# A two-layer trunk on one core: the products within chunks of its state-space mixer, issued for two chunks at once

## The chip, the core and the metric

The kernel runs on one core of a Trainium2 chip. The metric is the device time of one launch in microseconds (us); less is better. Time before: 2029.46 us, the median of 3 runs (2022.63 to 2030.07).

TensorE (PE; its weight loads are PEld) multiplies, VectorE (DVE) and ScalarE (ACT) and GpSimd (POOL) work on tiles in between, SyncE (SP) issues most transfers. Each engine takes its instructions in a fixed order; engines wait for each other by semaphores.

## What is computed

Layer 0 is a bidirectional state-space mixer (Mamba-2 form) on 256 context and 1024 latent tokens, layer 1 an attention mixer; each is wrapped in a normalisation with a modulation and a gated residual. The change lies in the mixer's scan, which splits the 1280 tokens into 10 chunks of 128. Cut to what matters:

```python
def ssd_scan(xs, dt, a, bm, cm, init_state, need_y=True):
    ...
    la_cum = jnp.cumsum(dtc * a, axis=2)
    ...
    causal = jnp.tril(jnp.ones((M_CHUNK, M_CHUNK), dtype=bool))[:, :, None, None]
    seg = la_cum[:, :, :, None] - la_cum[:, :, None, :]
    decay = jnp.exp(jnp.where(causal, seg, -jnp.inf))
    cb = jnp.einsum('bclgn,bcsgn->bclsg', cc, bc)
    w = cb[..., None] * decay * dtc[:, :, None]
    y_diag = jnp.einsum('bclsgr,bcsgrp->bclgrp', w, xc)
    y_off = jnp.einsum('bclgn,bcgrpn,bclgr->bclgrp', cc, prev, jnp.exp(la_cum))
    return (y_diag + y_off).reshape(xs.shape), final
```

`y_diag` is the product within chunks: for each chunk, group (8) and head (4 per group) a 128 x 128 matrix `w` times the chunk's inputs (64 columns per head). Both directions of the scan share `cb` and the inputs, so the kernel adds the two directions' decay matrices first and multiplies once.

## The kernel before, in words

The mixer's stage interleaves two streams. One projects: 48 tiles of 128 output columns, each in three blocks of tokens (256, 512, 512), in eight steps of the inner dimension, each step as three matmuls of operands split into a high and a low part (L168 to L170, tile `pj`). A convolution tile is evicted by ScalarE into `ub` (L636), goes through five taps on ScalarE and VectorE (L642, L645) and a Silu (L650). The other stream is `mix`, once per group when its four convolution tiles are there. For each of the 10 chunks it

- transposes inputs and B (`trans`, L690, tile `tc`) and copies them to `xst` and `Bt`;
- makes chunk states (`state`): GpSimd weighs the inputs (`xw`, L713), TensorE multiplies (L718, tile `st`), GpSimd and VectorE carry them on (`tm`, `PV`);
- makes the decay matrix (`wmat`): SP brings the cumulated logarithms per direction (`lab`, L750), GpSimd masks them (L754), ScalarE takes four exponentials per direction (L760, tile `W`), TensorE makes the cross product C times B (L770, tile `tc`), VectorE adds the directions (L773) and multiplies by the cross product (L775);
- multiplies the matrix with `xst` (`diag`, L791, tiles `yd`): four heads of 64 columns.

After the last chunk of a block of tokens (`inner`, L805) VectorE adds `yd` to the skipped inputs; `y_out` (L832, tile `yo`) adds what comes from earlier chunks and stores `y_d`, the input of the output projection.

The order on every engine is made ahead by `Plan.order`: a list scheduler with a rank, a planned duration and the engine for each step. A step starts at the earliest planned time at which the steps it needs have ended and its buffers are free; of those that could start, the lowest rank goes first. The steps of `mix` have ranks ahead of later projections. Buffers are counted as rings, taken in turn: `W0` and `W1` (the two directions' decay matrices) have two buffers each, `lab` three, `tc` two banks, `yd` one set of two banks per block of tokens. A `W0` buffer is taken by the first exponential of its direction and comes free when `diag` has ended (W0 also holds the sum), `W1` after the addition L773. What comes out is a fixed sequence per engine; on the chip an engine waits where the planned and the real durations differ.

Of the kernel before, what the change touches and what calls it, by code (L numbers as in the profile page):

```python
# [133 lines left out]
def tok0(c):  # L134
    return c * 128 + (2 if c >= 2 else 0)
# [6 lines left out]
def flat(ap):  # L142
    return ap.rearrange("p a b -> p (a b)")


def emit(tc, A, out):
    nc = tc.nc
    V, S, G, T, Q = nc.vector, nc.scalar, nc.gpsimd, nc.tensor, nc.sync
# [90 lines left out]
    def psum(tag, shape):  # L239
        return PS.tile(shape, FT, tag=tag, bufs=PSN[tag], name=tag)  # L240
# [424 lines left out]
    def mix(g, chs, rank):  # L665
# [6 lines left out]
        def op(eng, f, after, us, **kw):  # L672
            seq[0] += .01
            return plan.op(eng, f, after, rank + seq[0], us, **kw)

        s = {}
        hxst, hBt, hPV = plan.hold("xst"), plan.hold("Bt"), plan.hold("PV")
        ready, blocks = {}, {}
# [22 lines left out]
            d = op("ACT", lambda: S.activation(s["Bt"][:, c, :], t["p"][:, 2, :], AF.Copy), [a], .275, uses=[bank, hBt])  # L701
            ready[c] = (b, d)

        pv = [None]

        def state(i):
            bank, t, mms = plan.hold("st"), {}, []
# [31 lines left out]
        def wmat(c):  # L739

            t0, t, ws, bank = tok0(c), {}, [], plan.hold("tc")
            for d in range(2):
                hl, hw = plan.hold("lab"), plan.hold(f"W{d}")
                sgn = 1 - 2 * d

                def bring(d=d):
                    t["l", d] = pool["now"].tile([128, 4, 128], FT, tag="lab", bufs=NLAB, name="lab")
                    src = bass.AP(tensor=la_d.tensor, offset=la_d.offset + (c * 64 + d * 32 + g * 4) * 128,
                                  ap=[[0, 128], [1, 512]])
                    Q.dma_start(flat(t["l", d]), src)  # L750


                def close(d=d, sgn=sgn):
                    G.affine_select(t["l", d], t["l", d], [[0, 4], [sgn, 128]], OP.is_ge, NEVER, base=0,  # L754
                                    channel_multiplier=-sgn)

                def expo(h, d=d):
                    if h == 0:
                        t["w", d] = pool["now"].tile([128, 4, 128], FT, tag=f"W{d}", bufs=2, name="W")
                    S.activation(t["w", d][:, h], t["l", d][:, h], AF.Exp, bias=u_t[:, d, c, 4 * g + h:4 * g + h + 1])  # L760

                a = op("SP", bring, third + [la_op], .38, takes=[hl])
                a = op("POOL", close, [a], .88, uses=[hl])
                for h in range(4):
                    a = op("ACT", lambda h=h, f=expo: f(h), [a, u_op], .312, takes=[hw] if h == 0 else [], uses=[hl, hw], table="exp")
                ws.append((hw, a))

            def cross():
                t["cb"] = psum("tc", [128, 128])
                T.matmul(t["cb"], bt["a"][:, t0:t0 + 128], ct["a"][:, t0:t0 + 128], start=True, stop=True)  # L770

            b = op("PE", cross, [ab, ac], .22, takes=[bank], uses=[hb, hc])
            a = op("DVE", lambda: V.tensor_tensor(t["w", 0], t["w", 0], t["w", 1], op=OP.add), [w[1] for w in ws], .75,  # L773
                   uses=[w[0] for w in ws])
            a = op("DVE", lambda: V.tensor_tensor(t["w", 0], t["w", 0], t["cb"][:, None, :].to_broadcast([128, 4, 128]),  # L775
                                                  op=OP.mult), [a, b], .68, uses=[ws[0][0], bank])
            bi = [i for i, (c0, c1) in enumerate(BLOCKS) if c0 <= c < c1][0]
            if bi not in blocks:
                blocks[bi] = {"h": plan.hold("yd"), "ops": [], "c": BLOCKS[bi]}
                new = True  # L780
            else:
                new = False
            bk = blocks[bi]
            k = (c - bk["c"][0]) * 128

            def diag():
                if new:
                    bk["yd"] = [psum("yd", [128, 512]) for q in range(2)]
                for h in range(4):
                    q, j = divmod(h, 2)  # L790
                    T.matmul(bk["yd"][q][j * 64:(j + 1) * 64, k:k + 128], s["xst"][:, c, h, :], t["w", 0][:, h, :], start=True,  # L791
                             stop=True)

            bk["ops"].append(op("PE", diag, [a, ready[c][0]], .65, takes=[bk["h"]] if new else [], uses=[bk["h"], ws[0][0], hxst]))

        def inner(bi):

# [63 lines left out]
        for i in range(9):  # L861
            state(i)
            wmat(i)
            if i == 1:
                inner(0)
            if i == 5:
                inner(1)
        wmat(9)
        for q in range(2):
            y_out(0, q)  # L870
# [78 lines left out]
    for kind, g, q in ORDER:  # L949
        rank += 10  # L950
        if kind == "z":
            z_tile(next(zts), rank)
            continue
        chs.setdefault(g, []).append(conv_tile((2 * g, 2 * g + 1, 16 + g, 24 + g)[q], rank))
        mod_later(g, q, rank + LATE)
        if q == 3:
            mix(g, chs[g], rank + 1)
# [18 lines left out]
    with ExitStack() as st:  # L976
# [262 lines left out]
        a = plan.op("SP", norm_weights, [opened], HEAD, us=.76, small=True)  # L1239
# [3 lines left out]
        for i in range(2):  # L1243
# [9 lines left out]
            c = [plan.op("POOL", cosines, [scaled, b, *tabs], HEAD + 20 + 40 * i, 1.1)]  # L1253
# [299 lines left out]
    with ExitStack() as st:  # L1553
# [18 lines left out]
        held, shifts, brought, finished, last_scores, turns = {}, {}, {}, {}, [], []  # L1572
# [155 lines left out]
        for kt in range(KT):  # L1728
            for h in range(2):
                raw, t = plan.hold("wr"), {}  # L1730
                c = slice(h * 512, (h + 1) * 512)
# [10 lines left out]
                a = plan.op("SP", bring, [], R - 80 if kt < WE else 100 * NU - 150 + kt, takes=[raw])  # L1742
                a = plan.op("ACT", lambda t=t, f=part: S.activation(f(0), t["w"], AF.Copy), [a] + after, R, .63, uses=[raw])
# [151 lines left out]
```

## Time and profile before

| | us |
|---|---|
| median of 3 runs | 2029.46 |
| lowest and highest run | 2022.63, 2030.07 |
| the profiled execution | 2022.52 |
| its span, first to last instruction | 2020.8 |
| TensorE busy in it | 1959.8 (97%) |
| VectorE busy | 1433.7 (71%) |
| GpSimd busy | 1192.1 (59%) |
| ScalarE busy | 1109.0 (55%) |

The profile is of one execution. Busy time of TensorE counts each matmul from start to end, where neighbours overlap, so gaps shorter than a matmul's tail do not show as idle; start times in the timeline do show them. Mixer work with the changed products lies between 204 and 1004 us, the last projection of the stage at 1029, then the output projection and the attention layer follow.

### The profile page before, as it was taken

How to read it: one execution, taken by the hardware profiler on the slowest of the kernel's cores; microseconds unless marked ns; L12 is line 12 of the kernel's file. 1: busy time of each engine (PE TensorE's matmuls, PEld its weight loads, DVE VectorE, ACT ScalarE, POOL GpSimd, SP SyncE). 2: the span in 40 equal slices, each digit the busy share in tenths (PEclk: the TensorE clock that was granted, in tenths of full speed). 3: DMA queues.
4: the chain of work that ended last, by engine and by line, in shares of the span. 5: the costliest groups of instructions: out<-in, count | busy, mean ns of one | idle time of the engine just before them, and what ended most of it. 6: DMA issues, size and time to landing. Idle time of an engine off the chain costs nothing.

```text
span 2020.8 us, 30740 instructions
## 1 busy us (share of the span) xinstructions
PE 1959.8 (97%) x10728; PEld 1495.2 (74%) x10728; DVE 1433.7 (71%) x1737; ACT 1109.0 (55%) x2037; POOL 1192.1 (59%) x973
## 2 busy tenths in 40 slices
PE   8899999999999999999999999999998999999998
PEld 8778887888888888788878878887774444444476
DVE  1485888786959686776455788767574888888643
ACT  2447868576776668575644776543224445544521
POOL 1202767675847574755459787864264667776722
PEclk9999999999999999999999999999999999999999
DMA  6104455535363546354486685462233111111033
GB/s 243 63 32 127 142 171 149 155 98 170 113 189 102 157 118 175 123 147 153 140 277 213 214 257 188 155 180 94 74 94 89 32 37 43 48 43 37 6 103 105
DMA packets 163151, 255.51 MB, mean 126 GB/s; under 512 B 22490, under 2 KB 58202, under 8 KB 162996
## 3 DMA queue, kind: packets, MB, share of 16 engines
q1 hardware_dynamic: 161844, 251.71, 40.8%
q8 instruction: 84, 1.38, 0.3%
q10 hardware_dynamic: 1152, 1.84, 0.2%
q14 instruction: 71, 0.58, 0.1%
HBM read 210.78 MB, written 42.63 MB: 125 GB/s over the span
## 4 chain that ended last, share of the span: by engine, by line
PE 80%; DVE 7%; DMA 4%; ACT 3%; issue 2%; POOL 2%; SPq 1%; DVEq 0%; POOLq 0%; ACTq 0%
PE pj L168 9%; PE pj L169 8%; PE pj L170 8%; PE sc L1658 7%; PE ot L1674 7%; PE ob L168 7%; PE ob L170 7%; PE ob L169 7%; DVE acc L645 3%; PE yo L832 3%; PE st L718 3%; PE sc L1457 2%; PE yd L791 2%; DMA spare<-in_mod_w 2%; PE sc L168 1%
## 5 line engine op out<-in xcount | busy, mean ns | idle before, releaser
L168 PE MATMUL pj<-inh,whi 128*128 128x512 f32 (+1 forms) x1152 | 440.5, 382 | 3.9 <-DVE dv L453 3.2
L169 PE MATMUL pj<-inl,whi 128*128 128x512 f32 (+1 forms) x1152 | 409.7, 356 | 0.8 <-POOL inl L367 0.8
L170 PE MATMUL pj<-inh,wlo 128*128 128x512 f32 (+1 forms) x1152 | 410.4, 356 | 0.0
L754 POOL TENSOR_SCALAR_AFFINE_SELECT lab<-lab 128x512 f32<-128x512 f32 x160 | 150.6, 948 | 174.0 <-DMA lab<-la_d 135.3
L645 DVE SCALAR_TENSOR_TENSOR acc<-ub,convw,acc 128x1282 f32<-128x1282 f32 x128 | 232.5, 1817 | 18.8 <-ACT acc L642 15.8
L168 PEld LDWEIGHTS pj<-inh,whi 128*128 128x128 f32 x1152 | 219.0, 190 | 33.8 <-DVE dv L453 3.6
L170 PEld LDWEIGHTS pj<-inh,wlo 128*128 128x128 f32 x1152 | 218.3, 189 | 32.2
L169 PEld LDWEIGHTS pj<-inl,whi 128*128 128x128 f32 x1152 | 219.2, 190 | 26.2 <-POOL inl L367 1.2
L1639 POOL TENSOR_TENSOR acc<-acc,P 128x1024 f32<-128x1024 f32 x80 | 192.2, 2403 | 67.1 <-ACT P L1663 65.8
L1663 ACT ACTIVATE P<-sc 128x1024 f32<-128x1024 f32 x160 | 163.1, 1026 | 122.6 <-PE sc L1658 106.3
L760 ACT ACTIVATE W<-lab,u_t 128x128 f32<-128x128 f32 x640 | 201.4, 390 | 38.9 <-POOL lab L754 31.5
L1604 DVE TENSOR_REDUCE mx<-sc 128x2 f32<-128x1024 f32 (+1 forms) x140 | 167.4, 1214 | 40.9 <-PE sc L1457 39.9
L713 POOL TENSOR_TENSOR xw<-xst,te_t 128x256 f32<-128x256 f32 x144 | 142.0, 1003 | 43.0 <-DVE xst L697 16.5
L1674 PE MATMUL ot<-P,vv 128*64 128x512 f32 x640 | 156.5, 610 | 0.0
L1658 PE MATMUL sc<-q,kh 64*128 64x512 f32 x640 | 136.2, 422 | 6.5 <-ACT P L1663 3.9
L602 POOL TENSOR_TENSOR wlo<-wraw,whi 128x512 fp32r<-128x512 f32 x48 | 69.0, 1438 | 110.5 <-ACT whi L599 110.4
L1658 PEld LDWEIGHTS sc<-q,kh 64*128 64x128 f32 x640 | 60.2, 185 | 76.7 <-DVE mx L1604 29.5
L170 PE MATMUL ob<-whi,yl 128*128 128x512 f32 x288 | 113.4, 394 | 1.8 <-DVE yl L1056 1.4
L168 PE MATMUL ob<-whi,yh 128*128 128x512 f32 x288 | 113.9, 395 | 0.0
L169 PE MATMUL ob<-wlo,yh 128*128 128x512 f32 x288 | 112.9, 392 | 0.0
L732 POOL TENSOR_TENSOR tm<-PV,dec_t 128x512 f32<-128x512 f32 x64 | 97.0, 1515 | 25.4 <-DVE PV L736 25.4
L836 DVE TENSOR_TENSOR es<-yo,es 128x512 f32<-128x512 f32 (+1 forms) x96 | 53.2, 554 | 80.3 <-PE yo L832 44.5
(281 smaller groups left out, 4536.1 us busy)
## 6 DMA issues: line engine op xcount, KB each, us to landing
lab<-la_d SPq DMA_DIRECT2D x160, 256.0 KB
wraw<-in_w_in SPq DMA_DIRECT2D x96, 256.0 KB
workvv<-in_m_out_w SPq DMA_DIRECT2D x94, 256.0 KB
mraw<-in_mod_w SPq DMA_DIRECT2D x64, 256.0 KB
es<-e_d SPq DMA_DIRECT2D x128, 128.0 KB
wraw<-in_wqkv SPq DMA_DIRECT2D x48, 256.0 KB
spare<-in_mod_w SPq DMA_DIRECT2D x32, 256.0 KB
q_d<-qs SPq DMA_DIRECT2D x128, 64.0 KB
```

What stands on the lines that cost most here:

```text
L168: T.matmul(o, lh, rh, start=first, stop=False)
L169: T.matmul(o, lh, rl, start=False, stop=False)
L170: T.matmul(o, ll, rh, start=False, stop=last)
L645: V.scalar_tensor_tensor(t["a"], ub[i % 2][:, k:k + CW], convw[:, ct, k:k + 1], t["a"], op0=OP.mult, op1=OP.add)
L713: G.tensor_tensor(t[d], s["xst"][:, c], te_t[:, d, c, h4][:, :, None].to_broadcast([128, 4, 64]), op=OP.mult)
L754: G.affine_select(t["l", d], t["l", d], [[0, 4], [sgn, 128]], OP.is_ge, NEVER, base=0, channel_multiplier=-sgn)
L760: S.activation(t["w", d][:, h], t["l", d][:, h], AF.Exp, bias=u_t[:, d, c, 4 * g + h:4 * g + h + 1])
L1604: V.tensor_reduce(max_place(t["m"][0], i), o, AX.X, OP.max)
L1639: E.tensor_tensor(t[e], t["P", k0] if two else t[e], t["P", kt], op=OP.add)
L1658: T.matmul(o[:, h], (first_row[r] if n == 3 else (kh, kl, kh)[n][r, kv, k]), x[(0, 0, 1, 2)[n]][r], start=(n == 0), stop=(n == 3))
L1663: S.activation(t["P", kt], flat(t["s", kt]), AF.Exp)
L1674: T.matmul(t["o"][h * 64:(h + 1) * 64], vv[:, kt, kv], t["P", kt][:, h * 512:(h + 1) * 512], start=(kt == 0), stop=(kt == NT - 1))
```

## The change

`wmat` no longer issues `diag` for each chunk. It keeps the chunk in a list, and at every second chunk (odd `c`) it issues one step for both: eight products in a row, which needs both decay matrices and both copies of the inputs. The step's planned duration is 1.08 in place of .65 for one chunk, and it holds both `W0` buffers until it ends. Blocks of tokens start at even chunks, so a pair never spans two blocks. The number of products, their shapes and all other steps stay.

```diff
-        pv = [None]
+        pv, held = [None], []
...
             bi = [i for i, (c0, c1) in enumerate(BLOCKS) if c0 <= c < c1][0]
-            if bi not in blocks:
+            held.append((c, t, a, ws[0][0]))
+            if c % 2 == 0:
+                return
+
+            new, two = bi not in blocks, held[:]
+            held.clear()
+            if new:
                 blocks[bi] = {"h": plan.hold("yd"), "ops": [], "c": BLOCKS[bi]}
-                new = True
-            else:
-                new = False
             bk = blocks[bi]
-            k = (c - bk["c"][0]) * 128
 
             def diag():
                 if new:
                     bk["yd"] = [psum("yd", [128, 512]) for q in range(2)]
-                for h in range(4):
-                    q, j = divmod(h, 2)
-                    T.matmul(bk["yd"][q][j * 64:(j + 1) * 64, k:k + 128], s["xst"][:, c, h, :], t["w", 0][:, h, :], start=True,
-                             stop=True)
-
-            bk["ops"].append(op("PE", diag, [a, ready[c][0]], .65, takes=[bk["h"]] if new else [], uses=[bk["h"], ws[0][0], hxst]))
+                for c, t, _, _ in two:
+                    k = (c - bk["c"][0]) * 128
+                    for h in range(4):
+                        q, j = divmod(h, 2)
+                        T.matmul(bk["yd"][q][j * 64:(j + 1) * 64, k:k + 128], s["xst"][:, c, h, :], t["w", 0][:, h, :], start=True,
+                                 stop=True)
+
+            bk["ops"].append(op("PE", diag, [x for c, _, w, _ in two for x in (w, ready[c][0])], 1.08, takes=[bk["h"]] if new else [],
+                                uses=[bk["h"], hxst] + [x[3] for x in two]))
```

The scheduler makes a new order from this on every engine. On TensorE, in the third group of the mixer (before: chunks 6 and 7; `tc` is a cross product, `yd` the products within a chunk, four per chunk, `yo` a product with an earlier state), there stood:

```order
L770 MATMUL tc<-acc 128x128
L791 MATMUL yd<-W,xst 64x128 x4
L168 MATMUL pj<-inh,whi 128x512
L169 MATMUL pj<-inl,whi 128x512
L170 MATMUL pj<-inh,wlo 128x512
L791 MATMUL yd<-W,xst 64x128 x4
L770 MATMUL tc<-acc 128x128
L832 MATMUL yo<-acc,PV 128x128
```

and now, one set of projections earlier in the same group (chunks 4 and 5):

```order
L770 MATMUL tc<-acc 128x128
L795 MATMUL yd<-W,xst 64x128 x8
L837 MATMUL yo<-acc,PV 128x128
L168 MATMUL pj<-inh,whi 128x512
L169 MATMUL pj<-inl,whi 128x512
L170 MATMUL pj<-inh,wlo 128x512
```

Two short runs of `yd` with a set of projections between them have become one run of double length, of chunks two further back.

On ScalarE, in the same group around that place, with the tiles' numbers (before: W_4281 and W_4320 are W0 of chunks 8 and 9, W_4307 is W1 of chunk 8; `zs` and `acc` belong to projections):

```order
L660 ACTIVATE zs_4249<-pj_4196 128x512
L650 ACTIVATE acc_4148<-acc_4148,convb_82 128x1282
L760 ACT_TABLE_LOAD
L760 ACTIVATE W_4281<-lab_4188,u_t_100 128x128 x4
L760 ACTIVATE W_4307<-lab_4232,u_t_100 128x128 x4
L760 ACTIVATE W_4320<-lab_4247,u_t_100 128x128 x3
L660 ACT_TABLE_LOAD
```

and now (W_4239 and W_4259 are W0 of chunks 6 and 7, W_4176 and W_4277 their W1):

```order
L760 ACTIVATE W_4176<-lab_4102,u_t_100 128x128 x4
L660 ACT_TABLE_LOAD
L660 ACTIVATE zs_4206<-pj_4157 128x512
L650 ACTIVATE acc_4124<-acc_4124,convb_82 128x1282
L760 ACT_TABLE_LOAD
L760 ACTIVATE W_4239<-lab_4087,u_t_100 128x128 x4
L760 ACTIVATE W_4259<-lab_4146,u_t_100 128x128 x4
L760 ACTIVATE W_4277<-lab_4196,u_t_100 128x128
```

The W0 exponentials of both chunks of a pair now stand one behind the other, behind the pair before; a W1 has moved ahead of them.

## Rows read from the trace of the kernel before

**Rows 1.** The page's first part: busy us, share, instructions.

```profile
PE 1959.8 (97%) x10728; PEld 1495.2 (74%) x10728; DVE 1433.7 (71%) x1737; ACT 1109.0 (55%) x2037; POOL 1192.1 (59%) x973
```

**Rows 2.** Windows of 100 us: best, worst, and sum of the mixer's eight.

```profile
core 0: us, PE busy (x) PEld busy (x) DVE busy (x) ACT busy (x) POOL busy (x), PEclk, DMA share, GB/s
204.00:304.00 100.00, 99.89 (x609) 84.15 (x604) 86.66 (x101) 70.26 (x163) 70.17 (x67) 1.00 0.53 154
...
604.00:704.00 100.00, 96.97 (x583) 81.44 (x581) 82.09 (x91) 65.80 (x137) 66.38 (x55) 1.00 0.48 133
...
sum 800.00, PE 786.15 PEld 659.88 DVE 608.67 ACT 550.29 POOL 519.78; mean PE 98.27 PEld 82.49 DVE 76.08 ACT 68.79 POOL 64.97
```

**Rows 3.** Timeline of TensorE: start, us, line, tiles, rows*columns, size, count.

```profile
447.44 0.38 PE L770 MATMUL tc<-acc 128*128 128x128 f32 x2
447.75 0.66 PE L791 MATMUL yd<-W,xst 128*64 128x128 f32 x8
448.34 0.50 PE L168 MATMUL pj<-inh,whi 128*128 128x512 f32 x1
448.67 0.40 PE L169 MATMUL pj<-inl,whi 128*128 128x512 f32 x1
448.91 0.39 PE L170 MATMUL pj<-inh,wlo 128*128 128x512 f32 x1
449.23 0.66 PE L791 MATMUL yd<-W,xst 128*64 128x128 f32 x8
449.82 0.49 PE L770 MATMUL tc<-acc 128*128 128x128 f32 x2
450.14 0.39 PE L832 MATMUL yo<-acc,PV 128*128 128x128 f32 x2
```

**Rows 4.** Timeline of TensorE at the end of the mixer's stage.

```profile
1028.91 0.39 PE L169 MATMUL pj<-inl,whi 128*128 128x512 f32 x1
1029.14 0.40 PE L170 MATMUL pj<-inh,wlo 128*128 128x512 f32 x1
1029.37 0.40 PE L168 MATMUL tr<-whi,yh 128*128 128x512 f32 x1
```

**Rows 5.** Timeline of TensorE at one of four stretches of two chunks.

```profile
409.23 1.09 PE L791 MATMUL yd<-W,xst 128*64 128x128 f32 x16
410.25 1.13 PE L718 MATMUL st<-xw,Bt 128*128 128x256 f32 x4
411.22 0.38 PE L770 MATMUL tc<-acc 128*128 128x128 f32 x2
411.36 0.47 PE L168 MATMUL pj<-inh,whi 128*128 128x512 f32 x1
411.67 0.39 PE L169 MATMUL pj<-inl,whi 128*128 128x512 f32 x1
```

**Rows 6.** Line L791: matmuls, ns min/median/max; idle before it until (us, times).

```profile
L791 PE MATMUL yd<-W,xst x640: 272/273/324, 203.5 to 1003.0; 128*64 128x128 f32 x160
...
  ACT W L760: 2.4, 4
  DVE W L775: 1.3, 2
```

**Rows 7.** Timeline of ScalarE and VectorE at the same place as rows 3.

```profile
445.48 1.85 ACT L760 ACTIVATE W<-lab,u_t 128x128 f32<-128x128 f32 x6
...
447.36 0.69 DVE L773 TENSOR_TENSOR W<-W 128x512 f32<-128x512 f32 x1 [0.47 <-ACT W L760]
...
448.09 0.69 DVE L775 TENSOR_TENSOR W<-W,tc 128x512 f32<-128x512 f32 x1
```

**Rows 8.** Line L760: table loads, ns; idle before it until (us, times).

```profile
L760 ACT ACT_TABLE_LOAD  x53: 1283/1283/1283, 185.8 to 996.8; - x53
...
  PE yd L791: 11.4, 9
```

**Rows 9.** Line L770: idle before it until (us, times).

```profile
  DVE W L775: 10.7, 12
```

**Rows 10.** Timeline of TensorE: a cross product that waited for VectorE.

```profile
425.83 0.49 PE L770 MATMUL tc<-acc 128*128 128x128 f32 x2 [1.06 <-DVE W L775]
```

## The prediction

> **What bounds the kernel now.** I read the share of busy time and the granted clock first. TensorE is busy for 97% of the span, the next engine for 71% [rows 1], and its clock is at the full level (1.00 in all eight windows of the mixer, of which the best, the worst and the sum are shown, [rows 2]), so neither an idle engine nor the clock hides the change. The stage in which the changed products lie runs from about 204 to 1004 us. The table of windows shows that TensorE is busy for 786.15 of these 800 us while VectorE has 608.67 and ScalarE 550.29 [rows 2]: the stage is bound by the length of TensorE's own instruction stream, and 13.85 us are left in which it waits. So a change is worth what it takes out of that stream, less what it adds to the waits.
>
> Then I read the timeline of TensorE around the products within chunks (L791, tile yd). Projections (L168 to L170) follow each other every 0.23 us [rows 4]. In front of a yd stretch there is a gap, and behind one the next two instructions come late [rows 3].
>
> Last, I read where TensorE goes after the mixer: the last projection at 1029.14 is followed by the first product of the output projection at 1029.37, one step of 0.23 later [rows 4]. What the mixer's stream loses in length is therefore handed on to the end of the kernel; all the later stages are the same program.
>
> **The price of one stretch.** Instructions at 447.44 to 450.14 give it twice [rows 3]. First: the cross product (tc) starts at 447.44, yd follows, and the second projection behind it starts at 448.67, which is 1.23 us. The same sequence without yd stands at 411.22 to 411.67: 0.45 us [rows 5]. A stretch of 8 matmuls (one chunk) costs 0.78 us. Second: from the projection at 448.91 over yd and tc to yo at 450.14 is 1.23 us; without yd it would be 0.23 (one projection step) and 0.22 (tc to the next, 0.31 at 447.44 to 447.75 less the 0.09 of entering yd), again 0.78.
>
> The scheduler of before has by chance put two chunks side by side in four places, and one of them is at 409.23: 16 matmuls, 1.02 us to the next instruction against 0.59 for 8 (447.75 to 448.34) [rows 3, 5]. So the second 8 cost 0.43 us, and 0.78 - 0.43 = 0.35 us is paid for each stretch, whatever its length: some 0.09 on entering (0.32 against 0.23 at 448.91), 0.16 between the last yd and the next instruction, and 0.10 on the one after (0.33 against 0.23 at 448.34). The stretches differ from all around them in using 64 columns of the array (128*64 in their rows, 128*128 in the others).
>
> What the row shows here is that neighbours of the same shape overlap (projections are 0.23 apart though each lasts 0.39, [rows 4]) and that a border between shapes does not [rows 3]. The Trainium skill, "TensorE: Matmul & The Clock Gate", Part 2, step 4 (drain), says that the drain of one matmul overlaps the fill of the next, so that a stream costs only its columns; by that rule alone a border is free and the sum below would be 0 instead of 12.6 us. The trace agrees for the projections and not at these borders.
>
> **What the change removes.** The work is the same: 320 products in both orders, 640 instructions in the trace [rows 6]. Their stretches on TensorE, counted over the whole order, go from 76 (72 of one chunk, 4 of two) to 40 of two chunks. 36 fewer x 0.35 us = 12.6 us less of TensorE's stream. All other TensorE instructions are there in the same number, and the runs of other work between projections are 276 before and 279 now, so no new border of another kind pays this back.
>
> **What it adds and moves.** The first chunk's product waits for the second's decay matrix, and the wait stands on TensorE, where projections are queued behind it. Between the pairs of a group the order has 8 to 20 sets of three projections, so TensorE has something to run up to the place where the pair stands, but not beyond it. The matrices (W, two buffers per direction) of both chunks are now held until the pair is done, and ScalarE may write the next two only then. Behind that wait ScalarE has the evictions of the projections in its queue. ScalarE needs 0.31 us for each of the four exponentials of a chunk and direction (1.85 for 6), the sum and the product on VectorE 0.69 each [rows 7]: for the pair some 2.5 us of exponentials before the last two VectorE steps, then TensorE. In the order the mixer's last pair of a group falls 2 to 11 sets of projections (0.7 us each, three steps of 0.23) later than its last chunk did; the transposes that open the next group begin at the same set in every group, so the groups do not stretch. At the end of the mixer 25 sets follow the last pair where 32 followed the last chunk; 25 x 0.7 = 17 us still cover the additions and stores behind it. ScalarE's order has 10 table loads more, 10 x 1.283 = 12.8 us on an engine with 250 us to spare in the stage [rows 2, 8]: I cost it at nothing; what hides it is that TensorE waits for ScalarE's exponentials for 2.4 us in all [rows 6], and without that cover it would be at most these 12.8.
>
> The waits of TensorE are what I cannot count. Of the 13.85 us, VectorE's product of W and tc holds up the cross product for 10.7 in twelve places (a bank of tc comes free only then, [rows 9]), and yd itself waits 1.3 + 2.4 us for W [rows 6]; a place can be counted under two queues of TensorE, so these add up to slightly more than the idle time. The new order places all of these anew. Bounds from the windows: were all eight like the best one (0.11 idle), 0.9 us would be left and the kernel gain another 13.0; were all like the worst (3.03), 24.2 us, a loss of 10.4 [rows 2]. I take no change, since the same kinds of wait stand in the new order in the same number (80 cross products, 80 matrices) with half as many places where yd waits.
>
> **The sum.** -12.6 us, 0 for the waits, 0 elsewhere. Against the profiled execution (2022.52 us, span 2020.8) this gives 2009.9 us. That execution lies at the lower end of the runs shown: the median of the three is 2029.46, so the same sum there is 2016.9 us, and that is my number. 0.5% is 10.1 us and about what a measurement of this kernel can tell from no change; 12.6 is 0.62%, over it by 2.5 us alone.
>
> **Rivals.**
> - The waits eat it. For: the order is made from planned durations, not these, and a redrawn order keeps no wait where it was. At the price of the worst window everywhere it is -12.6 + 10.4 = -2.2: 2027.3 us. From 2.5 us of added waits on the verdict is "no change". Against: 13.85 us is little to begin with, and yd has half as many places to wait at.
> - The pair's border moves instead of going: the next stretch of full-width work pays for it, or a border is free and the gaps are something else. Then 2029.5. Against: the four double stretches pay it once [rows 5]. The rule on drains in "TensorE: Matmul & The Clock Gate" of the Trainium skill, Part 2, would have it so; the rows leave it little.
> - Slower: W's two buffers. Once a pair fills both, ScalarE can begin the next pair only after TensorE's product, so TensorE to ScalarE to VectorE to TensorE becomes a chain for each pair, and where the order has placed the next cross product or pair too early, TensorE stands. One of the longest such waits of now is 1.06 us (ahead of 425.83, [rows 10]). If each of the 40 pairs costs that, it is 42.4 us in place of the present 14.4, and the kernel ends at 2029.5 - 12.6 + 28.0 = 2044.9. It turns slower by over 0.5% from (12.6 + 10.1 + 14.4) / 40 = 0.93 us per pair on. For: ScalarE already waited 11.4 us for yd in nine places [rows 8]. Against: a pair comes about every 20 us (40 in 800), and the chain is some 6 us long (2.5 of exponentials, 1.3 of a table load, 1.4 on VectorE, 1.0 on TensorE).
>
> The Trainium skill, "Perfetto Trace Analysis", Optimization Strategy, warns that the same gap returning on the saturated engine can mean that buffers ran out; by it this rival would show as one gap per pair. No gap of that kind is on TensorE in the trace of before.
>
> **How the numbers follow.** Forecast (the borders go, the waits stay within +2.5 us or fall): 0.55. Waits eat it: 0.31. Border not gone: 0.04. The slower rival: 0.10. So faster 0.55, same 0.35, slower 0.10. For the range: below, the profiled level with the gain and half of the waits gone, 2009.9 - 6.9 = 2003; above, the median level with the worst waits, 2027.3, and a piece of the slow rival: 2029. What is left out is most of the slow rival and the cleanest case.
>
> **What would show it.** In the trace after: 40 stretches of 16 yd matmuls with 1.02 us to the next instruction and 0.09 of extra gap ahead (right), or stretches that are pulled apart by a wait (wrong). TensorE's busy time from the stage's start to the last projection shorter by some 12 us. The idle time of the stage near 14 us; 16.4 and more makes it "no change", 36 and more the slow rival, and then with cross products (L770) and yd waiting for W, and ScalarE's exponentials waiting for yd well over 11.4 us. The distance from the first product of the output projection to the end of the kernel must be the same as before; if it is longer, the gain was given back there, and the argument from [rows 4] is wrong.

## The result, and the profile after

The changed kernel takes 2015.11 us, the median of 6 runs (2010.65 to 2017.43), beside 2024.25 for 6 runs of the kernel before (2022.63 to 2030.07). The ratio is 0.9944 with an interval of 0.9933 to 0.9954: 0.56% faster, 11.3 us by the ratio and 9.1 by the two medians. The profiled execution of after (2017.43, span 2015.7) is as long as the slowest of the six, the one of before (2022.52, span 2020.8) just under the fastest of its six, so the two traces differ by 5.1 us only and show less of the gain than the runs do.

The page's first part, as [rows 1]:

```profile
PE 1953.1 (97%) x10728; PEld 1498.7 (74%) x10728; DVE 1433.2 (71%) x1737; ACT 1119.5 (56%) x2047; POOL 1189.5 (59%) x973
```

Same matmuls, 6.7 us less of TensorE; ScalarE has ten table loads more (2047 instructions against 2037). The windows of the mixer's stage, as [rows 2], the first of the eight and the sum (columns as there):

```profile
204.00:304.00 100.00, 97.61 (x610) 83.72 (x609) 89.52 (x105) 71.25 (x165) 73.07 (x68) 1.00 0.55 161
...
sum 800.00, PE 783.64 PEld 667.03 DVE 613.11 ACT 563.77 POOL 521.30; mean PE 97.95 PEld 83.38 DVE 76.64 ACT 70.47 POOL 65.16
```

TensorE is idle for 16.36 of these 800 us, 13.85 before. The first window has 2.28 of the difference of 2.51 (2.39 idle against 0.11); the other seven shift by up to 1.8 either way and nearly cancel.

TensorE's timeline at a pair in the third group, the place of [rows 3]:

```profile
446.72 0.38 PE L770 MATMUL tc<-acc 128*128 128x128 f32 x2
447.03 1.09 PE L795 MATMUL yd<-W,xst 128*64 128x128 f32 x16
448.06 0.49 PE L837 MATMUL yo<-acc,PV 128*128 128x128 f32 x2
448.30 0.48 PE L168 MATMUL pj<-inh,whi 128*128 128x512 f32 x1
448.62 0.40 PE L169 MATMUL pj<-inl,whi 128*128 128x512 f32 x1
```

There is one gap ahead of 16 products, 0.31 from tc where a border-free neighbour would come after 0.22; 1.03 later the next instruction follows. All 40 stretches of the trace are of 16, and their median time to the next instruction is 1.024. The end of the stage, as [rows 4]:

```profile
1023.40 0.40 PE L170 MATMUL pj<-inh,wlo 128*128 128x512 f32 x1
1023.64 0.40 PE L168 MATMUL tr<-whi,yh 128*128 128x512 f32 x1
```

The first product of the output projection starts at 1023.64, before at 1029.37 [rows 4]: 5.7 us earlier. From it to the last matmul it takes 982.7 us, before 982.0. What is gained is therefore gained in the mixer's stage and handed on.

The stage itself has become shorter by more than 5.7 us. TensorE's order is the same in both kernels up to some 200 us, and the same projection of 512 columns ahead of the mixer's products starts, before and then after, at

```profile
190.74 0.40 PE L168 MATMUL pj<-inh,whi 128*128 128x512 f32 x1
```

```profile
192.64 0.40 PE L168 MATMUL pj<-inh,whi 128*128 128x512 f32 x1
```

This execution of after was thus 1.9 us late before anything that was changed had run. From there to the first product of the output projection it takes 831.0 us, before 838.6: 7.6 us less.

Then who waits. The first view is of L795 (the products): its last two lines say who waited for it. The second is of L760 (the exponentials): its last two lines give the idle time ahead of it. Both as [rows 6, 8]:

```profile
L795 PE MATMUL yd<-W,xst x640: 272/273/324, 206.1 to 1002.9; 128*64 128x128 f32 x160
...
  issue: 7.6, 21
...
  ACT W L760: 19.9, 12
  DVE acc L810: 16.7, 13
```

```profile
L760 ACT ACT_TABLE_LOAD  x58: 1283/1283/1283, 187.7 to 993.3; - x58
...
  POOL lab L754: 42.0, 19
  PE yd L795: 19.9, 12
```

The products no longer wait for a decay matrix at all (2.4 + 1.3 us before, [rows 6]). ScalarE waits for them for 19.9 us, 11.4 before [rows 8]: the buffers of `W0` are indeed held longer. The cross product, which needs a bank that VectorE's L775 sets free, waits for it more than before (10.7 in [rows 9]):

```profile
  DVE W L775: 14.2, 19
```

### The profile page after: what moved, and what is told of

Same layout as the page of the kernel before. It is cut to its first block, busy times and chain, and to the rows that moved or that the text cites. A ratio compares the mean times of both kernels' runs of the same rounds, so it can differ in the third digit from the quotient of the medians.

```text
span 2015.7 us, 30716 instructions
## 1 busy us (share of the span) xinstructions
PE 1953.1 (97%) x10728; PEld 1498.7 (74%) x10728; DVE 1433.2 (71%) x1737; ACT 1119.5 (56%) x2047; POOL 1189.5 (59%) x973
## 4 chain that ended last, share of the span: by engine, by line
PE 73%; DVE 8%; DMA 7%; POOL 3%; ACT 3%; issue 3%; SPq 2%; DVEq 0%; POOLq 0%; ACTq 0%
PE pj L168 8%; PE pj L169 7%; PE pj L170 7%; PE sc L1663 7%; PE ot L1679 7%; PE ob L168 6%; PE ob L170 6%; PE ob L169 6%; DVE acc L645 3%; PE sc L1462 2%; PE yo L837 2%; PE st L718 2%; DMA spare<-in_mod_w 2%; DMA es<-e_d 2%; PE sc L168 1%
## 5 line engine op out<-in xcount | busy, mean ns | idle before, releaser
L169 PEld LDWEIGHTS pj<-inl,whi 128*128 128x128 f32 x1152 | 219.6, 191 | 26.6 <-POOL inl L367 1.2
L760 ACT ACTIVATE W<-lab,u_t 128x128 f32<-128x128 f32 x640 | 202.7, 391 | 64.6 <-POOL lab L754 42.0
L754 POOL TENSOR_SCALAR_AFFINE_SELECT lab<-lab 128x512 f32<-128x512 f32 x160 | 145.6, 915 | 153.5 <-DMA lab<-la_d 108.6
L713 POOL TENSOR_TENSOR xw<-xst,te_t 128x256 f32<-128x256 f32 x144 | 143.0, 1009 | 41.6 <-PE st L718 17.5
L902 DVE SCALAR_TENSOR_TENSOR macc<-mraw,cc,macc 128x512 f32<-128x512 f32 x98 | 101.2, 1058 | 11.1 <-DMA mraw<-in_mod_w 10.9
L732 POOL TENSOR_TENSOR tm<-PV,dec_t 128x512 f32<-128x512 f32 x64 | 92.5, 1446 | 17.8 <-DVE PV L736 16.7
```

The costliest lines, as they stand in the source:

```text
L169: T.matmul(o, lh, rl, start=False, stop=False)
L713: G.tensor_tensor(t[d], s["xst"][:, c], te_t[:, d, c, h4][:, :, None].to_broadcast([128, 4, 64]), op=OP.mult)
```

## The experiments

Three questions were left. Does the border between shapes pay, at 0.35 us each (theory A), or is it free and the gain an accident of the order (B)? Do the matrices that are held longer cost the kernel time (C), or does that wait lie off the path (D)? And why are 12.6 us of stream worth 9 to 11: because stream and waits hang together, or because the order of pairs waits less by itself, whatever its stream (E)? Where an expectation uses a letter without more, it is one of these. All medians below are of 5 to 12 runs. The kernel before, run beside them, had medians of 2024.63 (29 runs), 2024.82 (18) and 2024.08 (27). Where an edit leaves the planned durations alone (e1, e2, e5, e6, e9), the order of the other instructions stays as it is, and only the length of TensorE's stream changes.

**e1 and e2: a border measured by itself.** An identity product of 128 columns is added to each pair, in e1 ahead of its first chunk, in e2 between the two, where it cuts the stretch of 64-column products in two. The work is the same in both; the diff is e1's, in e2 the condition is `n == 1`.

```diff
-                for c, t, _, _ in two:
+                for n, (c, t, _, _) in enumerate(two):
                     k = (c - bk["c"][0]) * 128
+                    if n == 0:
+                        T.matmul(bk["yd"][0][:, k:k + 128], ident, ident, start=True, stop=True)
```

> The changed kernel with one more full-width product (identity times identity, 128 columns, two matmuls in the trace) written into the yd bank ahead of each pair; the pair's first product overwrites it, so the result stays. The order of all else is the same. It stands next to full-width work, so it adds no border. Theory A (each border pair around a 64-column stretch costs 0.35 us): 40 x 0.22 us (two matmuls of 0.11) = 8.8 us over the changed kernel (2015.1), some 2023.9. Rival B (borders are free, the gain came from a luckier order): the same 8.8 us; this run is the control for the next.

> The same extra product, now between the two chunks of each pair, so that each stretch of 16 is split in two by full-width work: 80 stretches as if chunks were issued singly, with the order of all else unchanged. Theory A: 40 x (0.22 + 0.35) = 22.8 us over the changed kernel, 2037.9, that is 14.0 us over the run with the product in front. Rival B: no difference to the run with the product in front, 2023.9.

Measured: e1 2020.61 (2018.01 to 2022.45), ratio 0.9979 [0.9969, 0.999]; e2 2028.09 (2025.72 to 2030.22), ratio 1.0024 [1.0015, 1.0033]. TensorE's timeline, e1 and then e2:

```profile
447.43 0.38 PE L770 MATMUL tc<-acc 128*128 128x128 f32 x2
447.65 0.39 PE L794 MATMUL yd<-ident 128*128 128x128 f32 x2
447.96 1.09 PE L797 MATMUL yd<-W,xst 128*64 128x128 f32 x16
448.99 0.49 PE L839 MATMUL yo<-acc,PV 128*128 128x128 f32 x2
```

```profile
447.72 0.38 PE L770 MATMUL tc<-acc 128*128 128x128 f32 x2
448.03 0.66 PE L797 MATMUL yd<-W,xst 128*64 128x128 f32 x8
448.62 0.49 PE L794 MATMUL yd<-ident 128*128 128x128 f32 x2
449.04 0.66 PE L797 MATMUL yd<-W,xst 128*64 128x128 f32 x8
449.63 0.49 PE L839 MATMUL yo<-acc,PV 128*128 128x128 f32 x2
```

From tc to yo it is 1.56 us in e1 and 1.91 in e2. The same products in one stretch more cost 0.35, as the prediction had it. All 40 pairs together, each taken from the instruction ahead of it to the one behind it, last 13.9 us longer in e2 than in e1, so this place is no exception; a free border (B) is ruled out. But 40 x 0.35 = 14.0 us of stream made the kernel only 7.5 us slower, and the 8.8 of e1 made it 5.5 slower; theory A had expected 2037.9 and 2023.9, all of the stream, and both came in under it. The sums of the eight windows, e1 and then e2, say where the rest went:

```profile
sum 800.00, PE 787.26 PEld 676.08 DVE 612.87 ACT 563.87 POOL 518.31; mean PE 98.41 PEld 84.51 DVE 76.61 ACT 70.48 POOL 64.79
```

```profile
sum 800.00, PE 791.03 PEld 669.63 DVE 608.69 ACT 558.90 POOL 516.69; mean PE 98.88 PEld 83.70 DVE 76.09 ACT 69.86 POOL 64.59
```

TensorE's idle time fell from 16.36 (after) to 12.74 (e1) and 8.97 (e2). With a longer stream TensorE stands idle for less: part of what was added fell into time in which it would have waited.

**e3 and e4: no `W0` to hold.** The exponentials write in place, into the `lab` buffers, of which there are 7 in one ring (the 3 + 2 + 2 of before); e3 is after with this, e4 before with this.

```diff
-NCH, NLAB = 6, 3
+NCH, NLAB = 6, 7
...
-                    if h == 0:
-                        t["w", d] = pool["now"].tile([128, 4, 128], FT, tag=f"W{d}", bufs=2, name="W")
+                    t["w", d] = t["l", d]
```

> The changed kernel, but the exponentials are written in place of their logarithms, and the seven buffers (three lab, two W0, two W1) form one ring: holding two chunks' matrices no longer keeps the next pair from starting. Theory C (the W0 pair that is held until both products are done gave back part of the gain): ScalarE's waits for yd fall from 19.9 us to under 3, TensorE's idle time in the eight windows from 16.4 to 10 or less, and the time by 4 to 8 us, to 2007 to 2011. Rival D (the waits are those of VectorE's product behind the masks' transfers, whatever W0 does): ScalarE's waits for yd fall as well, but the time stays within 3 us of 2015.

> The same buffers as in the run before this one, with the kernel before's single products per chunk. Theory A: 12.6 us slower than the pairs with these buffers (36 borders more or so x 0.35), less what waits differ. If the buffers alone bring something, it is slightly faster than the kernel before (2024.3): under C by 0 to 2 us only, since singly issued chunks never fill both W0 buffers for long (11.4 us of ScalarE's waits). Rival B: no steady difference between pairs and singles, since both orders are redrawn: within 4 us.

Measured: e3 2013.94 (2010.05 to 2017.3), ratio 0.9953 [0.9937, 0.9969]; e4 2028.36 (2024.57 to 2030.2), ratio 1.0019 [1.0009, 1.0029]. In e3, what ended the idle time ahead of the exponentials (now L759):

```profile
  POOL lab L754: 33.3, 25
  DMA lab<-la_d: 8.7, 3
```

ScalarE no longer waits for the products at all, where after has 19.9 us of that, and the time is after's within 1.2 us. By the bounds set ahead that is D and not C. But the order was drawn anew as well, and the first of the eight windows shows that it cost something there:

```profile
204.00:304.00 100.00, 92.83 (x550) 78.73 (x548) 90.75 (x106) 75.67 (x178) 78.76 (x69) 0.97 0.56 161
```

Of the 14.84 us for which TensorE is idle in e3, 7.17 lie in this window (2.39 in after), and the granted clock is 0.97 (1.00 in after). The other seven have 7.67 (13.97 in after), and the cross product waits less for VectorE (14.2 in after):

```profile
  DVE lab L774: 8.4, 11
```

So e3 by itself does not show that holding `W0` is free: a gain and a loss may have met. The clearer witness is e12, below. e4, in which 70 stretches are left, shows that the ring is no gain by itself. With the ring on both sides pairs are 14.4 us ahead, for 30 stretches less and with an order drawn anew on either side. Some of it is the clock: the mean granted clock of the runs is 0.9933 in e3 and 0.9916 in e4, which is an estimated 3.5 us of full-speed time if TensorE sets the pace throughout, and leaves some 11.

**e5 and e6: no borders at all.** Two products of 128 columns per chunk take the place of four of 64: both heads of a half are multiplied with the first one's matrix, so the computation is changed. e5 is before with this, e6 after.

```diff
-                for h in range(4):
-                    q, j = divmod(h, 2)
-                    T.matmul(bk["yd"][q][j * 64:(j + 1) * 64, k:k + 128], s["xst"][:, c, h, :], t["w", 0][:, h, :], start=True,
+                for q in range(2):
+                    T.matmul(bk["yd"][q][:, k:k + 128], flat(s["xst"][:, c, 2 * q:2 * q + 2, :]), t["w", 0][:, 2 * q, :], start=True,
                              stop=True)
```

> The kernel before, each chunk's four products of 64 columns replaced by two products of 128 columns (both heads of a half with the first head's matrix: this part of the computation is changed, so the time is that of a kernel without 64-column work). The order stands as before. The columns streamed are the same: two 64-column products run side by side, one of 128 columns takes as long, so a chunk is still some 0.44 us. Theory A (0.35 us for each stretch of 64 columns): 76 x 0.35 = 26.6 us less of TensorE's stream. If all of it reached the end, 1998; with the half to two thirds that reached it when products were added (5.5 of 8.8 and 7.5 of 14.0 us), 2007 to 2011. Rival B (the order's waits made the gain): no change against before, 2024.6.

> The changed kernel with the same replacement (two products of 128 columns per chunk, second heads multiplied by the first's matrix). Theory A: 40 x 0.35 = 14.0 us less of stream than the changed kernel, 7 to 14 us less time, 2001 to 2008, and the same time as the singly issued kernel with full-width products within 3 us: without borders it doesn't matter whether chunks go singly or in pairs. Rival B: the pairs' order is the better one by itself, so this stays 8 to 12 us under the singly issued one.

Measured: e5 2017.0 (2016.07 to 2024.15), ratio 0.9970 [0.9955, 0.9985]; e6 2008.23 (2003.0 to 2010.92), ratio 0.9925 [0.9911, 0.994]. TensorE's timeline of e5 shows a chunk without its border:

```profile
446.37 0.61 PE L790 MATMUL yd<-W,xst 128*128 128x128 f32 x4
446.74 0.48 PE L168 MATMUL pj<-inh,whi 128*128 128x512 f32 x1
```

A chunk's products take 0.37 to the next instruction (0.59 in [rows 3]). Over the ten stretches that stand between a cross product and a projection, the median from the cross product to the second instruction behind the stretch is 0.79 us by the start times of e5 and 1.13 by those of before: 0.34 for the border, a second measurement beside e2's. Against before, e5 takes 76 x 0.35 = 26.6 us out of the stream and gains 7.8; e6 takes 14.0 out of after's and gains 6.9. The sums of the windows, e5 and then e6:

```profile
sum 800.00, PE 774.92 PEld 667.86 DVE 614.69 ACT 551.43 POOL 525.78; mean PE 96.86 PEld 83.48 DVE 76.84 ACT 68.93 POOL 65.72
```

```profile
sum 800.00, PE 781.14 PEld 676.87 DVE 621.28 ACT 562.82 POOL 516.73; mean PE 97.64 PEld 84.61 DVE 77.66 ACT 70.35 POOL 64.59
```

Idle is 25.08 in e5 and 18.86 in e6, more than in before and after. The waits of TensorE's products in e5 (line waited for: us, times, longest):

```profile
PE tc L770 <- DVE W L775: 8.0, 10, 1.4
PE st L718 <- POOL xw L713: 5.8, 6, 1.4
```

In before the same two are 4.1 us in six places and 4.4 in five. TensorE comes sooner to steps for which VectorE and GpSimd are no sooner ready. e5 missed its 2007 to 2011 (of 26.6 us less stream under a third reached the end), and e6 lies just above its 2001 to 2008. e6 is 8.8 us ahead of e5 though neither has a border, where theory A expected the two within 3: with a stream this short, the order of pairs waits less, which speaks for E so far.

**e7: four at a time.** e3, with one step for all chunks of a block of tokens (2, 4 and 4), planned at 1.95 for four chunks: 24 stretches.

```diff
-            if c % 2 == 0:
+            if c not in (1, 5, 9):
                 return
```

> One ring of seven buffers as in the earlier run with pairs (2013.9), and the products issued once for each block of tokens (2, 4 and 4 chunks): 24 stretches for 40. Theory A: 16 x 0.35 = 5.6 us less of stream, 3 to 5.6 us less time, 2008.5 to 2011. Theory C (held matrices stall the chain behind them): four held matrices leave three of the seven buffers for the next block, ScalarE waits for yd more than 20 us again, and the time is 2014 or more.

Measured: 2031.15 (2025.4 to 2034.97), ratio 1.0033 [1.0018, 1.0049]: 17.2 us slower than e3, though 16 stretches fewer take 5.6 us out of the stream. Idle in the windows is 24.69 us (e3 14.84). The waits of TensorE's products in e7:

```profile
PE yo L836 <- DVE es L840: 13.1, 12, 3.4
PE st L718 <- DVE PV L736: 3.9, 3, 1.8
```

In e3 the first of these is 2.8 us in three places. ScalarE does not wait for the products here either. But the stage is not all of it. The two traces differ by 16.1 us, of which 2.9 lie ahead of the projection that the section on the result compares (189.84 in e3, 192.72 in e7), 7.1 between it and the first product of the output projection (1021.40 and 1031.34), and 6.1 behind that, where TensorE's order is the same in both. The clock is lower too, in the first window of the eight (0.97 in e3):

```profile
204.00:304.00 100.00, 90.91 (x543) 76.67 (x542) 85.51 (x100) 68.64 (x169) 73.71 (x67) 0.95 0.56 152
```

It is lower in the runs as well: their mean granted clock is 0.9904 in e7 and 0.9933 in e3, which is an estimated 6 of the 17.2 us if TensorE sets the pace throughout. In the stage, waits of `yo` for VectorE have grown by more than the borders give. That the long step put them off is likely but not shown: what share of it is the length of the step and what the order that happened to be drawn was not taken apart.

**e8, e10, e11, e12: the order drawn again.** Nothing but the planned duration of the products is changed, which makes the scheduler draw another order with the same work: before with .54 (e10) and .76 (e11) for .65, after with 1.30 (e8) and .90 (e12, the diff below) for 1.08.

```diff
-            bk["ops"].append(op("PE", diag, [x for c, _, w, _ in two for x in (w, ready[c][0])], 1.08, takes=[bk["h"]] if new else [],
+            bk["ops"].append(op("PE", diag, [x for c, _, w, _ in two for x in (w, ready[c][0])], .90, takes=[bk["h"]] if new else [],
```

> The changed kernel with the planned duration of a pair's step at 1.30 in place of 1.08 (twice the .65 of a single one). The work and the number of stretches (40) are the same; the order on all engines is drawn anew. Theory A: within 3 us of 2015.1, that is, what a redrawn order does by itself is small against the 12.6 us of borders. Rival B: the time moves by 6 us or more either way.

> The kernel before with the planned duration of a chunk's step at .54 in place of .65 (half of the pair's 1.08). Same work, 75 stretches, an order drawn anew. If before's order is an unlucky draw and the pairs' a lucky one: 2020 or less. If singles are slower by what they are: 2022 to 2027.

> The kernel before with the planned duration of a chunk's step at .76: another draw, 74 stretches. Same expectation: 2022 to 2027 if the number of stretches sets the time, 2020 or less if the draw does.

> The changed kernel with the planned duration of a pair's step at .90 in place of 1.08: another draw with 40 stretches, beside the one at 1.30 (2013.4). 2012 to 2018 if the number of stretches sets the time; 2020 and more if the draw does.

Measured:

| planned | one chunk at a time | stretches | pairs | stretches | difference |
|---|---|---|---|---|---|
| shorter | e10: 2018.92 (2014.35 to 2024.7) | 75 | e12: 2008.69 (2007.15 to 2011.35) | 40 | -10.2 |
| as written | before: 2024.08 to 2024.82 | 76 | after: 2015.11 (2010.65 to 2017.43) | 40 | -9.0 to -9.7 |
| longer | e11: 2021.75 (2015.43 to 2023.71) | 74 | e8: 2013.4 (2011.42 to 2016.29) | 40 | -8.4 |

The ratios to before are 0.9972 [0.9958, 0.9985] (e10), 0.9981 [0.9969, 0.9993] (e11), 0.9956 [0.9942, 0.997] (e8) and 0.9915 [0.99, 0.993] (e12). By the bounds set ahead e10 spoke for the draw ("2020 or less"), e11 lies between the two bounds, and e12 is below both of its own. What decides is the two sides together. The three draws of a side lie 5 to 6.4 us apart, so the draw is no small thing. The slowest order of pairs (2015.11) still lies under the fastest one of single chunks (2018.92), and the means differ by 9.2 us (2021.6 and 2012.4). e4 and e3 are a fourth order on each side and point the same way. So pairing is the cause and not the draw, though by the ratios the closest two, e8 and e10, have intervals that just overlap. Before and after were each the slowest of their three by the medians, so luck of the draw roughly cancels in the result. e12 is the fastest of the kernels with the computation unchanged, ahead of before by 0.85% and of after by 6.4 us between the medians (of two sets of runs, and its slowest run, 2011.35, lies just above the fastest of after, 2010.65). The sum of its windows:

```profile
sum 800.00, PE 791.53 PEld 678.19 DVE 613.43 ACT 569.50 POOL 510.50; mean PE 98.94 PEld 84.77 DVE 76.68 ACT 71.19 POOL 63.81
```

TensorE is idle for 8.47 us, half of after, while ScalarE waits even longer for the products to free `W0` (L795: who waited for it). A wait of this size can thus stand in the fastest of the kernels with the computation unchanged, and the cross product's wait for L775 is 5.6 us in it, where after has 14.2. This is what speaks for D:

```profile
  ACT W L760: 26.2, 16
```

**e9: the longer stream in the order of single chunks.** Before, with e1's identity product ahead of every second chunk: 40 products more.

```diff
             def diag():
                 if new:
                     bk["yd"] = [psum("yd", [128, 512]) for q in range(2)]
+                if c % 2:
+                    T.matmul(bk["yd"][0][:, k:k + 128], ident, ident, start=True, stop=True)
```

> The kernel before with the identity product (two matmuls of 0.11 us) ahead of every second chunk's products, in the same yd bank, overwritten behind it; the order of all else stays. It carries the same extra 8.8 us and about the same number of 64-column stretches (76 to 80) as the pairs that were split in the middle (2028.1): what differs is the order alone. Theory A (borders and their stream make the gain): 2028 to 2030, that is 3.5 to 5.5 us over before. Theory E (the pairs' order waits less by itself, as the full-width kernels with 8.8 us between them suggest): 2033 and more.

Measured: 2025.62 (2023.89 to 2029.66), ratio 1.0001 [0.9991, 1.0012]. The sum of its windows:

```profile
sum 800.00, PE 790.22 PEld 669.05 DVE 605.83 ACT 549.47 POOL 511.14; mean PE 98.78 PEld 83.63 DVE 75.73 ACT 68.68 POOL 63.89
```

The product costs 0.22 of stream each in e1 (1.56 against 1.34 from tc to yo), 8.8 us in all. It also splits the four double stretches of before: the trace has 80 stretches of 8, four more than before, another 1.4 us. For these 10.2 us the kernel is slower by 1.5 us by the medians and not at all by the ratio, and idle fell from 13.85 to 9.78. That is less than either expectation had (2028 to 2030 by A, 2033 and more by E). e2 has the same stream in the order of pairs (80 stretches of 8, 40 identity products) and is 2.5 us slower. So with a long stream the order of pairs is not the better one, and E falls as a general theory; what put e6 ahead of e5 shows only where the stream is short.

## Why the prediction was right, and by how much

*What bounds the kernel.* Right. The gain lies in the mixer's stage, and the distance from the first product of the output projection to the end is 982.7 against 982.0.

*The price of a stretch.* Right: 0.35 us by the trace of e2 against e1, 0.34 by e5 against before, 1.024 to the next instruction in after. The rival by which the border only moves fell with these rows. By "TensorE: Matmul & The Clock Gate" of the Trainium skill, Part 2, step 5 (the prediction names step 4), the drain of one matmul overlaps the fill of the next; the traces agree between projections and not where 64 and 128 columns meet. Another page of the Trainium skill, "TensorEngine Tiling (Array Packing)", Key Properties, says "Mode switching requires drain"; the rows fit that, at 0.35 us for going in and out, though none shows the drain itself.

*The sum.* 36 stretches of 0.35 us, 12.6, is the right length of stream and, as a forecast of time, somewhat too much: 9.1 to 11.3 were measured, and 9.2 over three orders a side. That the forecast of 2016.9 lies only 1.8 us above the 2015.11 is luck: it started from a median of three runs, 2029.46, that lies above the 2024 to 2025 of all later ones; from 2024.25 the sum would have given 2011.7, some 3.5 too low.

*The step that was off is "0 for the waits".* The products' own waits for a matrix went, others grew, and in all the idle time of the profiles rose from 13.85 to 16.36, at the edge of the 16.4 from which the text would have called it "no change". The mistake lies deeper: stream and waits are not separate terms. TensorE's waits depend on chains through VectorE, GpSimd and ScalarE, and e5 shows that these do not become shorter with its stream: its waits for L775 and L713 rose from 4.1 and 4.4 us to 8.0 and 5.8. Within one order the runs give:

| order | stream longer by, us | median, us | idle in the windows, us |
|---|---|---|---|
| pairs, e6 | -14.0 | 2008.23 | 18.86 |
| pairs, after | 0 | 2015.11 | 16.36 |
| pairs, e1 | +8.8 | 2020.61 | 12.74 |
| pairs, e2 | +22.8 | 2028.09 | 8.97 |
| single, e5 | -26.6 | 2017.0 | 25.08 |
| single, before | 0 | 2024.08 to 2024.82 | 13.85 |
| single, e9 | +10.2 | 2025.62 | 9.78 |

The lengths of stream are 0.35 for each border and 0.22 for each identity product, against the same order without the edit. Idle time goes against the stream in every row. In the order of pairs 36.8 us of stream moved the time by 19.9, some 0.54 us for each; in the order of single chunks the same 36.8 moved it by 8.6, some 0.23. How much of the gain is borders and how much the order of pairs can only be estimated from these. By e2 against e1, where 40 borders were worth 7.5 us, the 36 of the change would be worth 6.7, and the order 2 to 5; at the rate of single chunks, 12.6 x 0.23, the borders would be worth 2.9 and the order 6 to 8. That the order of pairs has no lead over e9 at e2's length of stream suggests that its part cannot be had by itself. Why single chunks answer so little to their stream stays open.

The 5.7 us between the two traces are 12.6, less 2.5 of idle, less the 1.9 by which this execution of after was late ahead of the stage, and less some 2.5 whose place stays open. A window of after ahead of the stage (columns as in [rows 2]):

```profile
100.00:150.00 50.00, 47.33 (x226) 38.94 (x227) 38.46 (x36) 23.76 (x30) 6.29 (x6) 0.90 0.11 37
```

The granted clock, here a mean of the full level (2.4 GHz, 1.00) and the lower one, is 0.90; before has 0.93 in the same window. In the 28 us ahead of it TensorE had idled for 2.24 us in after and 2.73 in before, and the clock was 1.00 in both. e8 runs the same instructions on TensorE there, and its clock in this window is 1.00:

```profile
100.00:150.00 50.00, 46.82 (x245) 38.77 (x244) 42.74 (x41) 23.45 (x29) 4.82 (x3) 1.00 0.10 32
```

The projection that starts at 192.64 in after starts at 187.79 in e8, 4.9 us sooner. So single traces differ by this much ahead of the change, and gains of this size are to be read from the medians of the runs.

*The rival "the waits eat it"* is the one that came nearest: it named the right mechanism, and the waits took, on balance, some 1.3 to 3.5 of the 12.6 us (12.6 less 11.3 and less 9.1), not the 10.4 it was priced at.

*The slower rival.* Its sign came: ScalarE waits for the products for 19.9 us in after and 26.2 in e12. Its price did not: the products never wait for a matrix in after, and e12 is the fastest of these kernels with the longer wait. The cross products' wait for VectorE did grow, by 3.5 us in after, and e3 leaves open whether the held buffers have a part in that; it is far from the 28 us of this rival. The argument against it, a chain of some 6 us in every 20, fits this. ScalarE's ten table loads, 12.8 us costed at nothing, were not tested by themselves; what can be said is that the products of after wait for no exponential.

## What to carry to other kernels

Changes between products of 64 and of 128 columns cost TensorE time of their own, here 0.35 us for each stretch, so products of the odd width belong together. How far is a question of what else waits: two chunks were right here, and the one order that was drawn for four was slower. Where the saturated engine has waits left, do not expect all that its stream loses: within one order a quarter to a half of it reached the end here. Measure the share once, by adding a known piece of work that changes no order. And where a scheduler draws the order, compare several draws on each side before a difference under 0.3% is believed, and keep the best.

## What the runs showed that was not expected

A planned duration changed by 0.11 to 0.18 us, with no work changed, moved the kernel by 2.3 to 6.4 us (e11, e10 and e12), up to more than half of what the change itself brings; the 1.7 us by which e8 lies under after is not clear of the spread of the runs. And adding work was nearly free: 40 more products and four more borders, 10.2 us of TensorE, in the order of single chunks cost 1.5 us by the medians and nothing by the ratio (e9), on an engine that is busy for 98% of that stage.
